# LayerNorm statistics from transposed copies with tokens on partitions

## The chip, the cores and the metric

The kernel runs on one core of a Trainium2 chip. The metric is the device time of one execution in microseconds (us). Six engines matter: PE (matrix products; its weight loads are listed apart as PEld), DVE (vector), ACT (scalar), POOL, and SP, which here only issues DMAs. Each engine works through its own queue in order; an instruction that waits holds up everything behind it on that engine.

## The reference

One inference step of a two-layer encoder over 512 prompt and 32 sample tokens, 1024 features, in float32. The part that the change touches is the end of each layer:

```python
u = x @ w_in                                   # split into three branches and three gates
...
merged = (jax.nn.sigmoid(ga) * (ya @ w_branch[0])
          + jax.nn.sigmoid(gb) * (yb @ w_branch[1])
          + jax.nn.sigmoid(gc) * (yc @ w_branch[2]))
r = ALPHA * x + merged @ w_out
r = r + jax.nn.sigmoid(r @ w_ple_gate) * (pe @ w_ple)
return layer_norm(r, ln_gain, ln_bias), ...
...
def layer_norm(x, g, b):
    mu = jnp.mean(xf, -1, keepdims=True)
    var = jnp.mean(jnp.square(xf - mu), -1, keepdims=True)
    y = (xf - mu) * lax.rsqrt(var + LN_EPS) * g + b
```

## The kernel before

Activations lie with features on partitions and tokens along the free dimension: 8 feature tiles of 128 x 544. Every float32 product is made of three products of a faster type (high and low parts of both operands: `xh`, `xl` and `wh`, `wl`), in `block` (L237), each in two halves of 272 tokens: 752 blocks of 128 x 128 weights in a layer, six matmuls each, 9,024 in all at L244. Weights come in chunks of eight blocks by DMA into `raw`; ACT and DVE split them (L200, L201), one unit ahead of PE.

The code is written out as units (`UNITS`): one unit is one feature tile of one product. Beside the units run jobs, Python generators whose `yield d` lets d ticks pass. A tick comes before each block, or before every second block where a product is made by halves. So jobs' instructions are put between matmuls at fixed places of each queue, and the numbers in `PACE` are those distances. Nothing is reordered on the chip.

A layer ends with units `wo` (output product), then `pg` (gate product), `pg` by halves from feature 6 in layer 0 and from feature 2 in layer 1 (`HELD`): first all these features for tokens 0 to 271, then all for 272 to 543. `evac` starts `gate` (L893) for each: ACT's sigmoid (L897, L899), DVE's product with `ple` (L901) and sum into r (L902). The normalization works along partitions. From the first two features PE makes a rough mean (`ln_center`, L714) that DVE and POOL subtract from all features (L718). Squares (ACT, L916) and running sums of values and squares (L918 to L928) follow. `ln_job` sums over partitions with PE (L737), makes A (power -1/2 on POOL, L745) and B on 128 partitions, spreads both over all partitions with PE (L752), and scales each feature in place (ACT L766, POOL L762, DVE L768 to L771). In layer 0 the result is split into `xh`, `xl` for layer 1, whose first units (`pl`) do not need it; in layer 1 it is stored with features on partitions (L774), and PE is given 30 and 5 matmuls on zeros (L262) around the last sums.

PSUM: two double-bank tiles for products (`mm`), two single banks `sc`, one `tp`, one `pv`.

Of the kernel before, what the change touches and what calls it, by code (L numbers as in the profile page):

```python
# [49 lines left out]
def blocks_of(kind):  # L50
# [11 lines left out]
WARM = (16, 30, 5)  # L62

PACE = {
# [53 lines left out]
def encoder(ctx: ExitStack, tc, xT, pT, W, RB, KC, VC, PAR, CST, o_y, o_k, o_v, o_rp, o_rs, o_cv, o_lr):  # L118
# [33 lines left out]
    mhalf = cp.tile([128, 3], F32, name="mhalf")  # L152
    warm = cp.tile([128, 1], F32, name="warm")
# [83 lines left out]
    def block(ps, xh, xl, first, last, hfs=(0, 1), n=None):  # L237
# [9 lines left out]
    def halves(ap):  # L247
        return ap.rearrange("p (a b) -> p a b", a=2)
# [32 lines left out]
    busy(WARM[0])  # L281
    V.memset(eps, EPS)
    V.memset(mhalf, -0.5)
    S.copy(warm, eps)
# [28 lines left out]
    def layer(l, env, nxt):  # L313
# [386 lines left out]
        def span(hf):  # L700
            return slice(0, N) if hf is None else slice(hf * H2, (hf + 1) * H2)

        def hfs_(hf):
            return (0, 1) if hf is None else (hf,)
# [4 lines left out]
        def ln_center():  # L709
            yield PACE["center"]  # L710
            c, s2 = tmp("center"), env["s2p"]
            for h in range(2):
                ps = psum("sc")
                T.matmul(ps[:, :H2], lhsT=cst[:, C_O1K:C_O1K + 128], rhs=env["acc"][:, span(h)])  # L714
                S.mul(c[:, span(h)], ps[:, :H2], 4.0)
            yield 2
            for f in (2, 3, 4, 5, 6, 7, 0, 1):
                (V if f < 4 else G).tensor_tensor(rt(f, None), rt(f, None), c, SUB)  # L718
            env["center"] = True
            yield 2  # L720
            S.activation(s2, rt(0, None), AF.Square)
            sq = tmp("sq")
            S.activation(sq, rt(1, None), AF.Square)
            yield 2
            G.tensor_tensor(s2, s2, sq, ADD)

        PIECES = [(c if i < 2 else H2 - 128, c, min(128, H2 - c), 0 if i < 2 else 128 - (H2 - c))
                  for i, c in enumerate((0, 128, 256))]

        def ln_job(hf):  # L730
            ones = cst[:, C_O1K:C_O1K + 1]
            if hf and l == L - 1:
                busy(WARM[1])
            ps = psum("tp")
            for q, src in enumerate((env["s1"], env["s2"])):
                for i, (c0, _, _, _) in enumerate(PIECES):
                    T.matmul(ps[:, 3 * q + i:3 * q + i + 1], lhsT=src[:, hf * H2 + c0:hf * H2 + c0 + 128], rhs=ones)  # L737
            if hf and l == L - 1:
                busy(WARM[2])
            w = sm.tile([128, 15], F32, tag="lnst", name="lnst", bufs=1)  # L740
            mu, e2, sq, A, B = (w[:, 3 * i:3 * i + 3] for i in range(5))
            V.tensor_copy(w[:, 0:6], ps[:, 0:6])
            V.tensor_tensor(sq, mu, mu, MUL)
            V.scalar_tensor_tensor(sq, e2, EPS, sq, ADD, SUB)
            G.tensor_tensor(A, sq, mhalf, ALU.pow)  # L745
            V.scalar_tensor_tensor(B, mu, -1.0, A, MUL, MUL)
            yield PACE[f"bc{2 * l + hf}"]
            AB = []
            for q, src in enumerate((B, A)):
                ps = psum("sc" if hf == 0 else "tp" if q == 0 else "pv")  # L750
                for i, (_, d0, n, i0) in enumerate(PIECES):
                    T.matmul(ps[:, d0:d0 + n], lhsT=bc(src[:, i:i + 1], [[0, 128]]), rhs=ident[:, i0:i0 + n])  # L752
                AB.append(ps[:, :H2])
# [340 lines left out]
```

## Time and profile before

| | us |
|---|---|
| runs | 1334.98 median of 3 (1334.26 to 1339.37) |
| profiled execution, its own time | 1333.96 |
| its span, first to last instruction | 1332.2 |
| PE / DVE / ACT / POOL busy | 1307.9 / 778.8 / 596.6 / 201.9 |

The span is what the trace covers; 1.8 us of the execution's time lie around it. A busy PE means matmuls in its pipeline, one starting about every 125 ns and each lasting about 290, so durations of matmuls overlap. The granted clock of TensorE is 1.00 at 2.4 GHz and 0.50 at 1.2 GHz; a stretch with a value between had both.

### The profile page before, as it was taken

Reading aid. Unit: us, or ns where it says so; the run is one execution under the profiler, and the core shown is the slowest. Engines: PE = TensorE matmul, PEld = TensorE weight load, DVE = VectorE, ACT = ScalarE, POOL = GpSimd, SP = SyncE. Lnnn points to the kernel's source line nnn. Section 1 sums busy time; section 2 is a strip of 40 time slices with the busy share of each in tenths; the row PEclk is TensorE's granted clock in tenths of the full one; section 3 lists DMA queues with packets and bytes.
Section 4 is the critical chain, followed back from the end, with each engine's and each line's share of the span. In section 5 each row is a group of like instructions: output and inputs, shape, how many; then the busy total and the mean of one; then the engine's idle time right before and its main releaser. Section 6 shows DMA issues by size and latency. Waiting matters only on the chain.

```text
span 1332.2 us, 26812 instructions
## 1 busy us (share of the span) xinstructions
PE 1307.9 (98%) x10783; PEld 1272.4 (96%) x10783; DVE 778.8 (58%) x1663; ACT 596.6 (45%) x1491; POOL 201.9 (15%) x192
## 2 busy tenths in 40 slices
PE   9999999999999999999999999999999999999985
PEld 9998899999999999999899998999999999999985
DVE  5666563673854444468884756547548545435587
ACT  6765544432642333334467654444245323333333
POOL 0210121320101101002312102133001110110034
PEclk9999999999999999999999999999999999999998
DMA  7233422221222222233112353232212222222201
GB/s 293 64 129 96 155 82 87 90 89 63 70 91 96 80 96 82 93 104 120 64 62 99 86 158 113 72 98 77 75 64 95 80 96 81 88 87 95 96 17 68
DMA packets 44285, 124.96 MB, mean 94 GB/s; under 512 B 9344, under 2 KB 13696, under 8 KB 43520
## 3 DMA queue, kind: packets, MB, share of 16 engines
q1 hardware_dynamic: 44160, 123.24, 28.3%
q8 instruction: 85, 1.39, 0.4%
q14 instruction: 40, 0.33, 0.1%
HBM read 111.52 MB, written 7.24 MB: 89 GB/s over the span
## 4 chain that ended last, share of the span: by engine, by line
PE 89%; DVE 6%; ACT 3%; issue 2%; POOL 0%; DVEq 0%; ACTq 0%; POOLq 0%
PE mm L244 78%; PE pv L413 2%; PE sc L386 1%; PE tp L402 1%; PE sc L639 1%; PE tp L322 1%; DVE held L201 1%; PE pv L653 1%; ACT wh L200 1%; PE mm L262 1%; DVE wl L201 1%; DVE r L718 1%; PE pv L657 1%; PE pv L497 0%; DVE s L923 0%
## 5 line engine op out<-in xcount | busy, mean ns | idle before, releaser
L201 DVE TENSOR_TENSOR wl<-raw,wh 128x256 fp32r<-128x256 f32 x704 | 306.6, 470 | 298.9 <-ACT wh L200 298.0
L244 PE MATMUL mm<-xh,wh 128*128 128x272 f32 x2144 | 455.4, 294 | 0.5 <-ACT xrp L833 0.5
L244 PE MATMUL mm<-xl,wh 128*128 128x272 f32 x2144 | 443.5, 288 | 0.0
L244 PE MATMUL mm<-xh,wl 128*128 128x272 f32 x2144 | 442.1, 287 | 0.4 <-DVE wl L201 0.4
L244 PEld LDWEIGHTS mm<-xh,wh 128*128 128x128 f32 x2144 | 334.3, 188 | 13.9 <-issue 9.9
L244 PEld LDWEIGHTS mm<-xh,wl 128*128 128x128 f32 x2144 | 335.9, 188 | 0.6 <-DVE wl L201 0.6
L244 PEld LDWEIGHTS mm<-xl,wh 128*128 128x128 f32 x2144 | 335.0, 188 | 0.0
L200 ACT CAST wh<-raw 128x256 fp32r<-128x256 f32 x704 | 251.0, 403 | 52.1 <-PE mm L244 49.3
L856 ACT ACTIVATE sg<-mm 128x544 f32<-128x544 f32 x48 | 30.0, 625 | 144.1 <-PE mm L244 144.1
L868 POOL TENSOR_TENSOR m<-m,sg 128x544 f32<-128x544 f32 x30 | 42.5, 1418 | 313.3 <-DVE sg L866 313.3
L244 PE MATMUL mm<-xh,held 128*128 128x272 f32 x320 | 64.8, 296 | 6.8 <-ACT sg L899 5.1
L347 ACT ACTIVATE sx<-sx,sst 128x128 f32<-128x128 f32 (+4 forms) x68 | 37.9, 558 | 66.7 <-DVE sst L345 63.9
L244 PEld LDWEIGHTS mm<-xh,held 128*128 128x128 f32 x320 | 51.6, 192 | 9.0 <-ACT sg L899 5.5
L244 PE MATMUL mm<-ml,wh 128*128 128x272 f32 x256 | 52.9, 288 | 0.0
L244 PE MATMUL mm<-mh,wl 128*128 128x272 f32 x256 | 52.8, 288 | 0.0
L244 PE MATMUL mm<-mh,wh 128*128 128x272 f32 x256 | 52.7, 287 | 0.0
L866 DVE TENSOR_TENSOR sg<-mm,sg 128x544 f32<-128x544 f32 x32 | 23.2, 725 | 41.3 <-PE mm L244 41.3
L255 ACT CAST xh<-r 128x544 fp32r<-128x544 f32 (+1 forms) x32 | 17.1, 533 | 66.6 <-DVE r L883 63.7
L244 PE MATMUL mm<-xl,held 128*128 128x272 f32 x160 | 46.6, 291 | 0.0
L244 PEld LDWEIGHTS mm<-mh,wl 128*128 128x128 f32 x256 | 40.1, 188 | 0.0
L244 PEld LDWEIGHTS mm<-mh,wh 128*128 128x128 f32 x256 | 40.1, 188 | 0.0
L244 PEld LDWEIGHTS mm<-ml,wh 128*128 128x128 f32 x256 | 40.0, 188 | 0.0
(257 smaller groups left out, 1855.1 us busy)
## 6 DMA issues: line engine op xcount, KB each, us to landing
raw<-in_W SPq DMA_DIRECT2D x189, 512.0 KB, 3.2
bias<-in_RB SPq DMA_DIRECT2D x16, 256.0 KB, 3.9
x<-in_xT SPq DMA_DIRECT2D x4, 544.0 KB, 8.9
o_v<-VA SPq DMA_DIRECT2D x2, 1088.0 KB, 5.6
o_k<-KT SPq DMA_DIRECT2D x2, 1088.0 KB, 5.2
swap<-KB SPq DMA_DIRECT2D x32, 68.0 KB, 2.8
swap<-QB SPq DMA_DIRECT2D x32, 68.0 KB, 2.0
o_y<-r SPq DMA_DIRECT2D x6, 272.0 KB, 2.2
```

Of the source, the lines that this page charges most:

```text
L200: S.copy(h, t)
L201: V.tensor_tensor(lo, t, h.bitcast(F32), SUB)
L244: T.matmul(ps[:, hf, :H2], lhsT=w[:, n % 2, :], rhs=x[:, hf * H2:(hf + 1) * H2], start=first and i == 0, stop=last and i == 2)
L255: S.copy(h, src)
L262: T.matmul(ps[:, 0, :H2], lhsT=zero[:, :128], rhs=zero, start=True, stop=True)
L322: T.transpose(tp[:rows, t * 128:(t + 1) * 128], src[:, t, c0:c0 + rows], ident)
L347: S.activation(x, x, AF.Exp, bias=s[:, 0:1], scale=-1.0, accum_out=s[:, 1:2])
L386: T.matmul(scs[j][:, o:o + n], lhsT=q_[r, p, i * 128:i * 128 + 128], rhs=k_[r, p, :n], start=k == 0, stop=k == 2)
L413: T.matmul(pv[64 * j:64 * j + 64, i * 128:i * 128 + 128], lhsT=env["vatok"][:, kt, h * 64:h * 64 + 64], rhs=xs[j][:, o:o + 128], start=kt ...
L856: S.activation(halves(sg), pv, AF.Sigmoid)
L866: V.tensor_tensor(halves(sg), pv, halves(sg), MUL)
L868: (V if kind == "bB" and t == 7 else G).tensor_tensor(m, m, sg, ADD)
```

## The change

Halves become tokens 0 to 287 and 288 to 543 (`SPANS`), so that they end with a token tile; the two parts lie side by side in PSUM, meeting at the bank's border. The statistics are made otherwise: PE transposes r, four feature tiles of one token tile into one `sc` bank (`turn`), and DVE takes BN_STATS over those 512 features (`stats`). That happens once per token tile for features 0 to 3 and once for 4 to 7; five token tiles, one of them with 32 tokens. BN_AGGR and one addition give mean and variance per token; POOL's power follows. Layer 0 goes on as before (A and B spread by PE, scaling with features on partitions). In layer 1 ACT also copies the transposed values to SBUF (`tk`), and the result is made from these with two scalar_tensor_tensor passes (`tok_ln`) with gain and bias spread over partitions by a DMA, and stored with tokens on partitions. For the very last token tiles features 4 to 6 are transposed and counted while the last unit runs, feature 7 after it, in banks `tp` and `pv`, and used from there. The centre, the squares, the running sums and the matmuls on zeros at the end go.

```diff
+SPANS = ((0, 288), (288, N))
+MM0 = 512 - SPANS[0][1]
+TILES = ((0, 128), (128, 256), (256, 288), (288, 416), (416, N))
+TILES_OF = ((0, 1, 2), (3, 4))
...
-WARM = (16, 30, 5)
+WARM = 16
...
+    "turn": 2, "tk": 1, "bc0": 3, "bc1": 4, "x": 5,
...
-                T.matmul(ps[:, hf, :H2], lhsT=w[:, n % 2, :], rhs=x[:, hf * H2:(hf + 1) * H2],
+                a, b = SPANS[hf]
+                T.matmul(ps[:, MM0 + a:MM0 + b], lhsT=w[:, n % 2, :], rhs=x[:, a:b],
...
-        def ln_center():
...
+        def turn(ps, c, f0, f1):
+            a, b = TILES[c]
+            for f in range(f0, f1):
+                T.transpose(ps[:b - a, f % 4 * 128:f % 4 * 128 + 128], env["r", f // 4][:, f % 4, a:b], ident)
+
+        def stats(ps, c, i, f0, f1):
+            n = TILES[c][1] - TILES[c][0]
+            V.bn_stats(bs[:n, c, i], ps[:n, f0 % 4 * 128:(f1 - 1) % 4 * 128 + 128])
+
+        def stats_job(hf, q):
+            for c in range(5) if hf is None else TILES_OF[hf]:
+                n = TILES[c][1] - TILES[c][0]
                 ps = psum("sc")
+                turn(ps, c, 4 * q, 4 * q + 4)
+                stats(ps, c, q, 4 * q, 4 * q + 4)
+                if last:
+                    env["tk", c, q] = tmp("tk", (128, 512))
+                    S.copy(env["tk", c, q][:n], ps[:n])
+                yield PACE["tk"]
+            if q:
+                add(ln_job(hf), 0)
+
+        def stats_end(t):
+            for c in TILES_OF[1]:
+                if t == 6:
+                    env["tk", c, 1] = psum("tp" if c == 3 else "pv")
+                ps = env["tk", c, 1]
+                turn(ps, c, *((4, 7) if t == 6 else (7, 8)))
+                stats(ps, c, 1 + t % 6, *((4, 7) if t == 6 else (7, 8)))
+                yield 0
+            if t == 7:
+                add(ln_job(1), 0)

         def ln_job(hf):
...
+            for i, c in enumerate(tiles):
+                n = TILES[c][1] - TILES[c][0]
+                V.bn_aggr(mv[:n, i], bs[:n, c, :3 if end else 2].rearrange("p a b -> p (a b)"))
+            V.tensor_scalar(e, mv[:, :, 1], EPS, None, ADD)
+            G.tensor_tensor(A, e, mhalf[:, :np_], ALU.pow)
+            if last:
+                yield from tok_ln(hf, tiles, mv, A, B)
+                return
+            V.scalar_tensor_tensor(B, mv[:, :, 0], -1.0, A, MUL, MUL)
+            yield PACE[f"bc{hf}"]
...
+        def tok_ln(hf, tiles, mv, A, B):
+            work = [(q, i, c) for q in range(2) for i, c in enumerate(tiles)]
...
+            for q, i, c in work:
+                n = TILES[c][1] - TILES[c][0]
+                x = env["tk", c, q][:n]
+                y = xs[q, i] = tmp("ty", (128, 512))[:n] if hf and q else x
+                V.scalar_tensor_tensor(y, x, mv[:n, i, 0:1], gain[:n, q], SUB, MUL)
+                if not hf:
                     yield 1
+            for q, i, c in work:
...
+                V.scalar_tensor_tensor(y, y, A[:n, i:i + 1], bias[:n, q], MUL, ADD)
+                Q.dma_start(out=o_y[a:b, 512 * q:512 * q + 512], in_=y)
+                if not hf:
+                    yield 1
...
             V.tensor_tensor(sg, sg, env["ple", t // 4][:, t % 4, span(hf)], MUL)
             V.tensor_tensor(r, r, sg, ADD)
...
+            if t == 3 or t == 7 and not (last and hf):
+                yield PACE["turn"]
+                add(stats_job(hf, t // 4), 0)
+            elif t in (6, 7) and last and hf:
+                add(stats_end(t), 2 * (t == 6))
...
+            if l + 1 == L and kind == "pg" and t == 0:
+                env["gb"] = sl("gb", shape=(128, 2048))
+                Q.dma_start(out=env["gb"], in_=bass.AP(LGB.tensor, LGB.offset, [[0, 128], [1, 2048]]))
```

DVE's queue at the end of layer 0, from the spreading of the first half's A to the second half's statistics. Before (`s_7685`, `s_7686` are the sums of values and squares, `lnA` is A spread):

```order
L755 COPY lnA<-sc 128x272
L768 TENSOR_TENSOR r<-r,lnA 128x272
L771 SCALAR_TENSOR_TENSOR r<-r,par_89,lnY 128x272
...
L256 TENSOR_TENSOR xl<-r,xh 128x272
L920 TENSOR_TENSOR s_7685<-s_7685,r 128x272
L923 TENSOR_TENSOR s_7686<-s_7686,sq 128x272
```

And now, the same place on DVE (`bst` takes the statistics, `lnst` mean, variance, A and B):

```order
L778 COPY lnA<-tp 128x288
L789 TENSOR_TENSOR r<-r,lnA 128x288
L790 SCALAR_TENSOR_TENSOR r<-r,par_89,lnY 128x288
L725 BN_STATS bst<-sc 128x6
L789 TENSOR_TENSOR r<-r,lnA 128x288
L790 SCALAR_TENSOR_TENSOR r<-r,par_89,lnY 128x288
L262 TENSOR_TENSOR xl<-r,xh 128x288
L725 BN_STATS bst<-sc 128x6
L790 SCALAR_TENSOR_TENSOR r<-r,par_89,lnY 128x288
L262 TENSOR_TENSOR xl<-r,xh 128x288
L760 BN_AGGR lnst<-bst 128x2 x2
L761 TENSOR_SCALAR lnst<-lnst 128x2
```

The second half's two BN_STATS and their sums now stand behind the first half's scaling steps. On PE, from the end of the first half's spreading, come 6 products, a group of four transposes, 6 products, another group, 36 products, and then the second half's spreading (L774); the products are those of `pl`, and 30 more follow.

PE's queue at the end of the kernel. Before (`zero` is the filling):

```order
L244 MATMUL mm<-xh,held 128x272
L262 MATMUL mm<-zero 128x272 x30
L737 MATMUL tp<-cst,s_15756 128x1 x3
L737 MATMUL tp<-cst,s_15757 128x1 x3
L262 MATMUL mm<-zero 128x272 x5
L752 MATMUL tp<-cst,lnst 128x128 x2
```

And now on PE, within the last unit and behind it:

```order
L253 MATMUL mm<-xh,held 128x256
L721 MATMUL tp<-cst,r 128x128 x3
L721 MATMUL pv<-cst,r 128x128 x3
L253 MATMUL mm<-xh,held 128x256
L253 MATMUL mm<-xl,held 128x256
...
L721 MATMUL tp<-cst,r 128x128
L721 MATMUL pv<-cst,r 128x128
```

Transposes of features 4 to 6 stand before the last six products, two of feature 7 behind them, and nothing of PE after that.

DVE's queue in the second half of layer 1, over its last two units. Before:

```order
L901 TENSOR_TENSOR sg<-sg,ple 128x272
L902 TENSOR_TENSOR r<-r,sg 128x272
L923 TENSOR_TENSOR s_15757<-s_15757,sq 128x272
...
L920 TENSOR_TENSOR s_15756<-s_15756,r 128x272
L923 TENSOR_TENSOR s_15757<-s_15757,sq 128x272
L742 COPY lnst<-tp 128x6
```

And now on DVE (L930 and L931 are the gate's product and sum, L814 the second pass of `tok_ln`):

```order
L814 SCALAR_TENSOR_TENSOR tk<-tk,lnst,gb 128x512
L814 SCALAR_TENSOR_TENSOR tk<-tk,lnst,gb 32x512
L930 TENSOR_TENSOR sg<-sg,ple 128x256
L931 TENSOR_TENSOR r<-r,sg 128x256
L725 BN_STATS bst<-tp 128x6
L725 BN_STATS bst<-pv 128x6
...
L807 SCALAR_TENSOR_TENSOR tk<-tk,lnst,gb 128x512 x2
L807 SCALAR_TENSOR_TENSOR ty<-tp,lnst,gb 128x512
L807 SCALAR_TENSOR_TENSOR ty<-pv,lnst,gb 128x512
```

The first half's passes now stand in front of feature 6's gate, whose sum the last unit's transposes on PE need.

## Rows read from the trace of the kernel before

**Rows 1.** The page, part 1: busy us (share of the span) xinstructions
```profile
PE 1307.9 (98%) x10783; PEld 1272.4 (96%) x10783; DVE 778.8 (58%) x1663; ACT 596.6 (45%) x1491; POOL 201.9 (15%) x192
```
**Rows 2.** Waits of PE: who waited for whom: us in total, times, longest us
```profile
PE mm L244 <- ACT sg L899: 5.1, 2, 3.1
...
PE tp L737 <- DVE s L920: 1.5, 2, 1.1
```
**Rows 3.** Stretches: length, busy us of each engine (instructions), PEclk, DMA share, GB/s
```profile
217.00:237.00 20.00, 20.00 (x167) 19.92 (x166) 8.96 (x15) 10.26 (x23) 5.76 (x5) 1.00 0.34 96
618.00:684.00 66.00, 63.03 (x477) 61.05 (x475) 56.32 (x106) 35.51 (x88) 26.54 (x24) 0.97 0.16 54
660.00:670.00 10.00, 9.61 (x67) 9.61 (x68) 7.49 (x21) 6.54 (x15) 1.80 (x3) 0.83 0.01 2
1264.00:1290.00 26.00, 22.10 (x157) 21.04 (x156) 22.78 (x40) 11.71 (x33) 10.48 (x8) 0.93 0.07 23
```
**Rows 4.** Chain of waits, 350 to 640: start us, us, what
```profile
355.87 261.80 PE mm L244 x2088
617.67 0.92 PE sc L714 x4
```
**Rows 5.** PE's timeline, first of six L497: start, us, engine line op, names, shapes
```profile
44.50 0.29 PE L497 MATMUL sc<-xch,held 128*128 128x274 f32 x1
...
45.26 0.42 PE L244 MATMUL mm<-xh,wh 128*128 128x272 f32 x2
```
**Rows 6.** PE's timeline at an existing group of four transposes
```profile
219.47 0.60 PE L322 MATMUL tp<-cst,VB 128*128 128x128 f32 x4
219.83 0.50 PE L244 MATMUL mm<-xh,wh 128*128 128x272 f32 x2
220.16 0.41 PE L244 MATMUL mm<-xl,wh 128*128 128x272 f32 x2
```
**Rows 7.** PE's timeline, sums over partitions and spreading, layer 1, first half
```profile
1293.11 1.45 PE L737 MATMUL tp<-cst,s 128*128 128x1 f32 x12
...
1297.51 1.41 PE L752 MATMUL sc<-cst,lnst 128*128 128x128 f32 x12
```
**Rows 8.** PE's timeline, two waits and the last product (idle before, releaser)
```profile
1280.40 0.47 PE L244 MATMUL mm<-xh,held 128*128 128x272 f32 x1 [3.12 <-ACT sg L899]
...
1309.24 0.39 PE L244 MATMUL mm<-xh,held 128*128 128x272 f32 x1 [1.95 <-ACT sg L899]
...
1312.24 0.29 PE L244 MATMUL mm<-xh,held 128*128 128x272 f32 x1
```
**Rows 9.** Groups of DVE by form: count | busy us, mean ns | idle before
```profile
L487 DVE SCALAR_TENSOR_TENSOR xc<-xrp,par,xc 128x547 f32<-128x547 f32 x24 | 18.9, 787 | 4.1 <-ACT xc L485 3.5
L352 DVE TENSOR_SCALAR sx<-sx,sst 128x512 f32<-128x512 f32 x16 | 9.4, 590 | 0.6
L418 DVE COPY ya<-pv 128x512 f32<-128x512 f32 x8 | 5.5, 688 | 5.2 <-PE pv L413 5.2
L744 DVE SCALAR_TENSOR_TENSOR lnst<-lnst 128x3 f32<-128x3 f32 x4 | 0.7, 164 | 0.1
```
**Rows 10.** Timeline of POOL and DVE, layer 0's first half being scaled
```profile
654.02 5.67 POOL L762 TENSOR_TENSOR r<-r,lnA 128x272 f32<-128x272 f32 x6 [0.77 <-DVE lnA L755]
654.53 0.82 DVE L771 SCALAR_TENSOR_TENSOR r<-r,par,lnY 128x272 f32<-128x272 f32 x1
657.14 1.00 DVE L768 TENSOR_TENSOR r<-r,lnA 128x272 f32<-128x272 f32 x1
```
**Rows 11.** Timeline of ACT, DVE and POOL behind the last product
```profile
1314.03 0.38 ACT L899 ACTIVATE sg<-mm 128x272 f32<-128x272 f32 x1
1315.21 0.44 DVE L902 TENSOR_TENSOR r<-r,sg 128x272 f32<-128x272 f32 x1
1318.85 0.86 POOL L745 TENSOR_TENSOR lnst<-lnst,mhalf 128x3 f32<-128x3 f32 x1 [4.32 <-DVE lnst L744]
1325.15 3.96 DVE L771 SCALAR_TENSOR_TENSOR r<-r,par,lnY 128x272 f32<-128x272 f32 x7
```

More of the change, by code (lines that the diff above doesn't have):

```diff
@@ L280, in encoder @@
     V.memset(zero.bitcast(F32), 0.0)
-    busy(WARM[0])
+    busy(WARM)
     V.memset(eps, EPS)
     V.memset(mhalf, -0.5)
+    V.memset(lnst, 0.0)
     S.copy(warm, eps)
@@ L700, in span @@
         def span(hf):
-            return slice(0, N) if hf is None else slice(hf * H2, (hf + 1) * H2)
-        def hfs_(hf):
-            return (0, 1) if hf is None else (hf,)
+            return slice(0, N) if hf is None else slice(*SPANS[hf])
+        last = l == L - 1
         def rt(f, hf):
             return env["r", f // 4][:, f % 4, span(hf)]
-        def ln_center():
-            yield PACE["center"]
-            c, s2 = tmp("center"), env["s2p"]
-            for h in range(2):
-                ps = psum("sc")
[L714 to L725, printed above, removed]
@@ L727, in layer @@
-        PIECES = [(c if i < 2 else H2 - 128, c, min(128, H2 - c), 0 if i < 2 else 128 - (H2 - c))
-                  for i, c in enumerate((0, 128, 256))]
-        def ln_job(hf):
[L731 to L747, printed above, removed]
+        bs = bst[:, l]
@@ new lines, in stats_end @@
+        def stats_end(t):
[8 more added lines that the diff above has]
+                add(ln_job(1), 0)
+        def ln_job(hf):
+            tiles = TILES_OF[hf]
+            end = last and hf
+            np_ = len(tiles)
+            w = lnst[:, l, hf]
+            mv, e, A, B = w[:, :2 * np_].rearrange("p (a b) -> p a b", b=2), w[:, 6:6 + np_], w[:, 9:9 + np_], w[:, 12:12 + np_]
+            for i, c in enumerate(tiles):
[8 more added lines that the diff above has]
+            yield PACE[f"bc{hf}"]
@@ L748, in ln_job @@
             AB = []
+            first = SPANS[hf][0]
             for q, src in enumerate((B, A)):
[L750 to L753, printed above, removed]
+                ps = psum("sc" if hf else "tp" if q else "pv")
+                for i, c in enumerate(tiles):
+                    a, b = TILES[c]
+                    T.matmul(ps[:, a - first:b - first], lhsT=bc(src[:b - a, i:i + 1], [[0, 128]]),
+                             rhs=ident[:b - a, :b - a])
+                AB.append(ps[:, :SPANS[hf][1] - first])
@@ L756, in ln_job @@
             yield 1
-            last = l + 1 == L
-            while hf and not last and ("x", 7, 0) not in nxt:
+            while hf and ("x", 7, 0) not in nxt:
                 yield 1
-            pooled = range(3, 8) if last and hf else range(2, 8)
-            for f in pooled:
+            for f in range(2, 8):
                 G.tensor_tensor(rt(f, hf), rt(f, hf), A, MUL)
@@ L779, in ln_job @@
                     nxt["x", e, hf] = True
-                if not last:
-                    yield 1 + f % 2
-                elif not hf:
+                yield 1 + f % 2
+        def tok_ln(hf, tiles, mv, A, B):
+            work = [(q, i, c) for q in range(2) for i, c in enumerate(tiles)]
+            gain, bias = (env["gb"][:, k * 1024:k * 1024 + 1024].rearrange("p (a b) -> p a b", a=2) for k in range(2))
+            xs = {}
+            for q, i, c in work:
[6 more added lines that the diff above has]
+            for q, i, c in work:
+                a, b = TILES[c]
+                n = b - a
+                y = xs[q, i]
+                V.scalar_tensor_tensor(y, y, A[:n, i:i + 1], bias[:n, q], MUL, ADD)
+                Q.dma_start(out=o_y[a:b, 512 * q:512 * q + 512], in_=y)
+                if not hf:
                     yield 1
@@ L875, in evac @@
                     env["ple", t // 4] = sl("ple")
-                S.copy(halves(env["ple", t // 4][:, t % 4]), pv)
+                S.copy(env["ple", t // 4][:, t % 4], pv)
             elif kind == "wo":
@@ L895, in gate @@
             sg = tmp("sg")[:, span(hf)]
-            if hf is None:
-                S.activation(halves(sg), ps[:, :, :H2], AF.Sigmoid)
-            else:
-                S.activation(sg, ps[:, hf, :H2], AF.Sigmoid)
+            S.activation(sg, ps[:, MM0:MM0 + N][:, span(hf)], AF.Sigmoid)
             yield 1
```

84 lines of the change are left out of this document (26 added, 58 removed), and 1 row of the table PACE.

## The prediction

> **What bounds the kernel now.** I read the engine shares first, then TensorE's waits, then busy time and granted clock by stage, then the timeline of the slow places. PE is busy 1307.9 of the 1332.2 us span [rows 1], so outside a few stretches time is what PE must issue, plus where it stands. It stands longest, 5.1 us, for the gate's sigmoid (L899, in layer 1) and 1.5 us for a running sum (L920, in layer 0) [rows 2]. Both belong to the end-of-layer normalization, and that is where all the slack lies: over 618 to 684 us PE is busy 63.03 of 66 us, so 3.0 idle, and over 1264 to 1290 us 22.10 of 26, so 3.9 idle; and the granted clock is 0.83 over 660 to 670 and 0.93 over 1264 to 1290 us [rows 3], which is 0.17 x 10 = 1.7 us and 0.07 x 26 = 1.8 us of full-speed time (part of the latter while PE stands; I count 1.5). And from the end of the last product (1312.24 + 0.29 = 1312.53, [rows 8]) to the end of the span lie 19.7 us in which one chain over all engines runs: filling matmuls, sums, power, broadcast, eight features in place, stores.
>
> **The change, part by part.**
> *PE work.* Added: 80 transposes, 18 groups of four (10 in layer 0, 8 in layer 1) before the last eight. An old group of four starts at 219.47, the next product at 219.83, and that pair then takes 0.33 instead of 0.25 us [rows 6]: 0.36 + 0.08 = 0.44 us a group, 18 x 0.44 = 7.9 us. Removed: the mean's matmuls, 0.92 us a layer [rows 4], 1.8; the twelve passes of sums, 1.45 us [rows 7], three times before the tail, 4.4; the broadcast's twelve passes of layer 1's first half, 1.4 [rows 7]; four of the twelve passes of layer 0's second half, 0.5. Sum 8.1. Net **-0.2 us**.
>
> *The split 288 + 256 for 272 + 272.* All 9,024 products (4,512 pairs) change shape. 2,088 products of 272 columns take 261.80 us, 125.4 ns each [rows 4]; six of 274 take 45.26 - 44.50 = 0.76 us, 127 ns [rows 5]. So a column costs, and 288 + 256 cost what 544 cost before: **0**. Bounds: were the time set by columns alone it would be exactly 0 (a gain has no source); were 256 columns held at the pace of 272 (no row shows fewer columns under a full 128x128 load of this type) and 288 paid 125.4 x 16/272 = 7 ns more, the price is 4,512 x 7 ns = 32 us. Matmuls with one column, whose pace only the weight load can set, start every (1.45 - 0.25)/11 = 109 ns [rows 7], the last pass taken at 0.25 us, below the 118 ns expected for 256. I take 0, by that nearest row.
> The Trainium skill ("TensorE: Matmul & The Clock Gate", LDWEIGHTS (loading the stationary operand)) gives a weight load as its columns over 1.2 ns, 107 ns for 128, which is also what 256 columns take at 2.4 GHz: no slack is left, which speaks against this split. The 109 ns agrees with it; by the page the load just still hides, and the sum stays.
>
> *Layer 0.* The subtraction of the centre goes (4 on DVE, 4 on POOL), squares and running sums too; ten BN_STATS of 512 columns come, not in the trace. Nearest row: a DVE copy of 128x512 from PSUM, 688 ns [rows 9]; bounds 0.59 (the same width as tensor_scalar from SBUF, [rows 9]) and 1.4 (two such passes). I take 0.69. Lost before: 3.0 idle + 1.7 clock = 4.7 us. What is late next: PE's second broadcast (L774; here L774, L789, L790 and L262 are lines of the new code). From the end of the first one PE issues 48 products and two groups of transposes, 48 x 0.125 + 0.88 = 6.9 us. DVE in that time, in its queue order: copy of A 0.44, L789 0.44, L790 0.82, BN_STATS 0.69, L789 1.0, L790 0.82, L262 1.0, BN_STATS 0.69, L790 0.49, L262 0.43; POOL's six multiplications make the two-operand ones that slow (0.82 and 1.00 between 654.02 and 659.69, [rows 10]). With 0.3 us to begin, 7.1 us; two BN_AGGR and the addition at the length of other tiny operations (0.16, [rows 9]) 0.5; the power 0.86 [rows 11] and two handovers 0.4; B 0.2; so 9.2 us. PE stands 2.3 to 2.8 us, taken as 2.8, and I count another 1.5 us for a clock drop as behind the wait of 3.12 us. With 0.4 for small waits that stay, 4.7 against 4.7: **0**. Queued behind it on PE: 30 products for ple, then layer 1's first; nothing else waits.
>
> *Layer 1, first half.* The sigmoid stood in ACT's queue behind a square that waited for the centre's subtraction: 3.12 us at 1280.40 [rows 8], most of the 3.9 idle. No centre, no such wait; with the clock 1.5 that is 5.4; I leave 0.4 for new waits on a DVE that still splits weights. **-5.0 us**.
>
> *Layer 1, second half.* The 1.95 us at 1309.24 [rows 8] go the same way. New: DVE applies the first half's normalization, twelve scalar_tensor_tensor over 512 columns (a 32-row tile costs as much). The row of this form, 547 columns with a column operand, is 787 ns [rows 9]; 0.75 for 512. From the first tile's statistics (24 x 0.118 + 0.44 + 0.3 = 3.6 us after the half begins) to feature 6's sum DVE has 5 x 0.69 + 5 gates x 0.9 (product and sum, [rows 11]) + 0.7 small + 12 x 0.75 = 17.7 us: done at 21.4 with 0.1 of gaps. PE reaches feature 6's transposes after 138 products of 118 ns and five groups: 18.5 us. It stands **2.9** us, with 18 of the last unit's products done and 6 queued behind, and six more transposes cost 0.75. -1.95 + 2.9 + 0.75 = **+1.7 us**.
>
> *The tail.* From the last product: sigmoid 0.42, product and sum 0.96 [rows 11], two transposes 0.44, two BN_STATS of 128 columns 0.48, two BN_AGGR and one addition 0.5: 2.8 us. Then eight passes of 0.75 = 6.0; the power (0.86) runs beside the first four. The last store: before, DVE ended at 1325.15 + 3.96 = 1329.11 [rows 11], 3.1 us ahead of the span's end; four stores of 256 KB follow each other now, so 3.5. Sum 12.3 against 19.7: **-7.4 us**.
>
> *At nothing:* the load of gain and bias (1 MB) sits in SP's queue between weight loads that come once per 6 us unit; three follow it. ACT's eight copies replace eight squares and eight lnY. If that cover fails, one weight load is about 3 us late.
>
> Sum: -0.2 + 0 + 0 - 5.0 + 1.7 - 7.4 = -10.9 us against the profiled execution's 1333.96 (span 1332.2): 1323.1. The median of the runs is 1.0 higher, so about **1323 to 1324; I say 1323.5**.
>
> **Rivals.**
> 1. *Slower: 256 columns no longer hide the weight load.* Place: every pair. At the bound of 32 us the time is 1334 - 11 + 32 = 1355. It decides from 4 ns a pair (18 us: 1341). For it: no row below 272; against: 109 ns above. 0.08.
> 2. *No change: VectorE is the bound at the end.* BN_STATS at 1.4 us: five in the second half (+3.5), two at the layer boundary (+1.4), 2 x 0.2 in the tail, and feature 6 late by as much again where POOL or ACT hand over late: +6, 1329 to 1330. For it: DVE is loaded in both stretches; against: single-operand reads from PSUM are 688 ns. 0.12.
> 3. *Faster still: DVE keeps up,* neither new wait appears (2.9 + 2.5 + 1.5): 1316 to 1317. For it: my queue sums carry small gaps; against: twelve passes of 0.75 do not shrink. 0.20.
> 4. *The transposes cost clock.* If groups between products count as idling, the clock halves at the four clusters, 1.5 us each: +6, 1329. Against: 217 to 237 us hold five such groups at a clock of 1.00 [rows 3]. The Trainium skill (same page, Part 4: PE-mode transpose) says that the full clock does not engage for transposes, since they do not count as busy; the trace does not bear that out for groups between products. 0.05.
>
> Forecast (both new waits as above, within some 3 us): 0.55.
>
> **How the numbers follow.** Predicted 1323.5, the forecast's own range 1320 to 1328. The range holds rival 3 (low end 1314, with passes at 0.69 as well) and most of rivals 2 and 4, and 1 or 2 ns a pair: 1314 to 1332. Measurement tells from no change about 0.5%, here 6.7 us: faster is below 1328.3, slower above 1341.7. Faster: 0.55 + 0.20 + 0.02 of rivals 2 and 4 = 0.77; same 0.15; slower 0.08.
>
> **What the profile after would show.** PE: pairs of 288 and 256 starting 0.25 us apart together; groups of four transposes 0.36 us long; a wait of 2 to 3 us before layer 0's second broadcast, with a clock below 1 behind it; no wait for the sigmoid; about 3 us before feature 6's transposes. DVE: BN_STATS of 512 near 0.69 us, passes near 0.75. Last product to end: about 12 us instead of 19.7. The prediction is wrong if pairs take more than 254 ns, if PE waits for the statistics' PSUM buffers (DVE late by more than two tiles), or if the tail stays above 15 us.

## The result

The kernel after takes 1319.38 us (median of four runs, 1318.69 to 1319.66), the kernel before 1336.37 us (median of four, 1334.26 to 1339.37): a ratio of 0.987, 95% interval 0.985 to 0.989. The profiled executions went from 1333.96 to 1319.27 us, 14.7 us less where the working said 10.9, and their spans from 1332.2 to 1317.2. The medians lie 17.0 us apart, since executions of the kernel before vary more, from 1333.94 us at a mean granted clock of 0.993 to 1339.61 at 0.988 (the four of the kernel after have 0.996 or 0.997), and the profiled one is among the fastest. Faster was right. The time lies in the stated range of 1314 to 1332, 0.6 us below the forecast's own 1320 to 1328, between the forecast and rival 3. The sum was 4 us short, and single terms were off by up to 3.4 us, because some errors cancel.

### The profile page after: what moved, and what is told of

It is laid out like the page before. It is cut to its first block, busy times and chain, and to the rows that moved or that the text cites. A ratio compares the mean times of both kernels' runs of the same rounds, so it can differ in the third digit from the quotient of the medians.

```text
span 1317.2 us, 26576 instructions
## 1 busy us (share of the span) xinstructions
PE 1299.4 (99%) x10744; PEld 1265.1 (96%) x10744; DVE 757.1 (57%) x1649; ACT 581.5 (44%) x1447; POOL 164.4 (12%) x158
## 4 chain that ended last, share of the span: by engine, by line
PE 81%; DVE 4%; ACT 2%; issue 1%; DVEq 0%; POOL 0%; ACTq 0%
PE mm L253 72%; PE pv L420 1%; PE tp L409 1%; PE sc L393 1%; PE sc L646 1%; PE tp L329 1%; PE pv L660 1%; PE pv L664 1%; PE sc L583 0%; ACT wh L208 0%; PE sc L721 0%; PE sc L476 0%; DVE tk L807 0%; DVE tk L814 0%; DVE xl L262 0%
## 5 line engine op out<-in xcount | busy, mean ns | idle before, releaser
L253 PE MATMUL mm<-xh,wh 128*128 128x288 f32 x2144 | 457.9, 295 | 0.4 <-ACT xrp L866 0.4
L253 PE MATMUL mm<-xh,wl 128*128 128x288 f32 x2144 | 444.1, 288 | 0.0
L253 PE MATMUL mm<-xl,wh 128*128 128x288 f32 x2144 | 442.7, 288 | 0.0
L253 PEld LDWEIGHTS mm<-xh,wl 128*128 128x128 f32 x2144 | 328.6, 188 | 0.0
L208 ACT CAST wh<-raw 128x256 fp32r<-128x256 f32 x704 | 251.0, 403 | 53.1 <-PE mm L253 49.3
L253 PE MATMUL mm<-xh,held 128*128 128x288 f32 (+1 forms) x320 | 64.0, 291 | 0.3 <-ACT ple L908 0.3
L253 PE MATMUL mm<-mh,wh 128*128 128x288 f32 (+1 forms) x256 | 52.8, 288 | 0.0
L253 PE MATMUL mm<-mh,wl 128*128 128x288 f32 (+1 forms) x256 | 52.8, 287 | 0.0
L253 PE MATMUL mm<-ml,wh 128*128 128x288 f32 (+1 forms) x256 | 52.8, 287 | 0.0
L253 PE MATMUL mm<-xl,held 128*128 128x288 f32 (+1 forms) x160 | 46.4, 290 | 0.5 <-DVE xl L262 0.4
L261 ACT CAST xh<-r 128x544 fp32r<-128x544 f32 (+2 forms) x32 | 17.0, 531 | 67.5 <-DVE r L915 63.5
```

What stands on the lines that cost most here:

```text
L208: S.copy(h, t)
L253: T.matmul(ps[:, MM0 + a:MM0 + b], lhsT=w[:, n % 2, :], rhs=x[:, a:b], start=first and i == 0, stop=last and i == 2)
L261: S.copy(h, src)
```

## The profile after

The page of the kernel after, part 1 (busy us, share of the span, instructions), to lay beside [rows 1]:

```profile
PE 1299.4 (99%) x10744; PEld 1265.1 (96%) x10744; DVE 757.1 (57%) x1649; ACT 581.5 (44%) x1447; POOL 164.4 (12%) x158
```

PE is busy 8.5 us less in a span 15 us shorter. The waits of PE in the kernel after, to lay beside [rows 2]:

```profile
PE tp L721 <- DVE r L931: 2.0, 2, 1.4
PE sc L774 <- DVE lnst L766: 1.5, 1, 1.5
...
PE mm L253 <- DVE xl L262: 0.4, 1, 0.4
```

The sigmoid is gone from the list. Both waits that the prediction expected in its place are there, each shorter than forecast: before layer 0's second broadcast (L774) 1.5 us for 2.8, and before feature 6's transposes 0.6 for 2.9 (the other 1.4 of L721 is in the tail, where PE has only feature 7's transposes left). In PE's timeline:

```profile
665.36 1.16 PE L774 MATMUL sc<-cst,lnst 128*128 128x128 f32 x8 [1.47 <-DVE lnst L766]
...
1304.74 0.33 PE L721 MATMUL tp<-cst,r 128*128 128x128 f32 x1 [0.61 <-DVE r L931]
```

The stretches of [rows 3], in the kernel after:

```profile
217.00:237.00 20.00, 20.00 (x165) 19.94 (x165) 9.13 (x14) 9.38 (x21) 4.39 (x4) 1.00 0.36 110
618.00:684.00 66.00, 63.66 (x502) 62.16 (x500) 45.19 (x103) 31.40 (x77) 12.69 (x14) 1.00 0.18 58
660.00:670.00 10.00, 8.53 (x70) 8.31 (x69) 8.62 (x21) 7.92 (x18) 5.81 (x8) 1.00 0.00 1
1264.00:1290.00 26.00, 26.00 (x206) 25.93 (x205) 16.14 (x38) 10.83 (x31) 0.00 (x0) 1.00 0.09 32
```

The sixth figure from the left behind the length is the granted clock: it is 1.00 in all four rows, and the 0.83 and 0.93 of the kernel before are gone. The last row also holds three groups of four transposes between products. The Trainium skill ("TensorE: Matmul & The Clock Gate", Part 4: PE-mode transpose) says that the full clock does not engage for transposes; for groups of four among products this trace shows the clock at 1.00.

To see where the time went I cut both traces at the same four products. PE's timeline of the kernel before, at the start of layer 0's first gate product, of layer 1's first product over both halves and of layer 1's first gate product (the last product is in [rows 8]):

```profile
598.72 0.42 PE L244 MATMUL mm<-xh,wh 128*128 128x272 f32 x2
...
684.69 0.52 PE L244 MATMUL mm<-xh,wh 128*128 128x272 f32 x2 [0.46 <-ACT xrp L833]
...
1252.10 0.41 PE L244 MATMUL mm<-xh,wh 128*128 128x272 f32 x2
```

The same three and the last product in the kernel after:

```profile
600.89 0.41 PE L253 MATMUL mm<-xh,wh 128*128 128x288 f32 x2
...
684.34 0.52 PE L253 MATMUL mm<-xh,wh 128*128 128x288 f32 x2 [0.41 <-ACT xrp L866]
...
1252.80 0.42 PE L253 MATMUL mm<-xh,wh 128*128 128x288 f32 x2
...
1305.84 0.28 PE L253 MATMUL mm<-xh,held 128*128 128x256 f32 x1
```

The table gives the five pieces, in us of the profiled executions, for these two kernels and those of the experiments below. A and C hold no normalization, B is the boundary of the layers, D the last gate units, E the tail from the last product's start. Where the code of a piece is the same, A differs between kernels by up to 1.7 us, B to E by 0.7 at most.

| kernel | A: to 1st gate | B: to layer 1 | C: to 2nd gate | D: to last product | E: to the end | span |
|---|---|---|---|---|---|---|
| before | 598.7 | 86.0 | 567.4 | 60.1 | 19.9 | 1332.2 |
| after | 600.9 | 83.4 | 568.5 | 53.0 | 11.4 | 1317.2 |
| e1 split only | 599.9 | 87.7 | 568.8 | 60.9 | 18.8 | 1336.1 |
| e2 no centre | 599.5 | 86.0 | 567.5 | 53.0 | 19.7 | 1325.7 |
| e3 no token form | 600.6 | 83.4 | 568.4 | 56.6 | 16.4 | 1325.4 |
| e4 broadcast later | 600.8 | 83.7 | 568.9 | 53.1 | 11.4 | 1317.8 |
| e5 broadcast earlier | 600.4 | 86.4 | 568.4 | 53.1 | 11.4 | 1319.6 |
| e6 double statistics | 601.6 | 83.4 | 568.4 | 56.2 | 11.5 | 1321.0 |
| e7 all at the end | 599.9 | 83.5 | 569.1 | 51.6 | 12.2 | 1316.2 |
| e8 wide 272 | 598.9 | 83.3 | 567.8 | 53.0 | 11.4 | 1314.4 |
| e9 e7 and e8 | 599.0 | 83.3 | 568.3 | 51.5 | 12.2 | 1314.3 |
| e10 one column | 600.4 | 86.6 | 569.1 | 53.0 | 11.5 | 1320.6 |

## The experiments

**e1 and e8: what the split costs.** e1 gives the kernel before the columns 288 and 256:

```diff
-                T.matmul(ps[:, hf, :H2], lhsT=w[:, n % 2, :], rhs=x[:, hf * H2:(hf + 1) * H2],
+                a, b = SPANS[hf]
+                T.matmul(ps[:, MM0 + a:MM0 + b], lhsT=w[:, n % 2, :], rhs=x[:, a:b],
...
-            pv = ps[:, :, :H2]
+            pv = ps[:, MM0:MM0 + N]
```

> The kernel before with one part of the change alone: products cut into 288 and 256 columns (and the product's PSUM buffer read as one stretch of 544 columns); the old statistics stay, cut at column 288 too. My step: the split costs nothing, at most 3 us in all (0.65 ns for each of 4,512 pairs, which is what the milestones of the two traces leave for it), so 1336 to 1339 us, with pairs starting 0.250 to 0.252 us apart. Rival 1 of the prediction: 256 columns no longer hide the weight load, 7 ns a pair, +32 us, about 1368. The second half of the last layer has six passes fewer (the broadcast needs two pieces of tokens, not three), which is worth 0.5 us.

Measured: 1338.82 against 1336.12 us, a ratio of 1.0017 (1.0006 to 1.0027), 0.8 to 3.6 us slower. Rival 1 with its 32 us is dead, but the term is not 0. In the profiles e1 is 3.9 us longer, and that is not all the split's price: A and C hold 2.6 of it, and 1.7 are in B, where the old sums over partitions now stand behind a longer wait and the clock falls once more. Twelve passes of one column behind a wait of PE, first in e1, then in the kernel before, each with a stretch of 5 us around them:

```profile
649.77 1.50 PE L741 MATMUL tp<-cst,s 128*128 128x1 f32 x12 [0.66 <-DVE s L924]
650.00:655.00 5.00, 5.00 (x32) 5.00 (x32) 2.16 (x8) 0.42 (x1) 1.62 (x2) 0.66 0.00 0
```

```profile
648.34 1.50 PE L737 MATMUL tp<-cst,s 128*128 128x1 f32 x12 [0.35 <-DVE s L920]
648.00:653.00 5.00, 4.66 (x39) 4.66 (x40) 2.20 (x9) 1.04 (x4) 1.38 (x2) 1.00 0.00 0
```

The clock at 0.66 over 5 us costs 0.34 x 5 = 1.7 us. e8 gives the kernel after equal halves again wherever both halves run at once:

```diff
-                a, b = SPANS[hf]
-                T.matmul(ps[:, MM0 + a:MM0 + b], ...
+                (a, b), m0 = (SPANS[hf], MM0) if len(hfs) == 1 else ((hf * H2, hf * H2 + H2), 512 - H2)
+                T.matmul(ps[:, m0 + a:m0 + b], ...
...
```

> The kernel after, but all products that run over both halves at once are cut 272 and 272 again; 288 and 256 are kept where the two halves are computed one after the other (the last six features of layer 0 and six of layer 1, and the first two products of layer 1). The split alone was 2.7 us slower than the kernel before (0.8 to 3.6). Theory A: that is the price of a pair of unequal columns, in every pair; it comes back: 2 to 2.5 us faster than the kernel after, 1316.5 to 1317.5, and layer 1 from its first wide product to its first gate takes 567.4 us in place of 568.5. Theory B: the price sits in the stretches by halves, and in other code: no change, 1319.

Measured: 1316.41 us (1316.17 to 1316.81), 3.0 below the kernel after, ratio to before 0.986 (0.984 to 0.987); A and C fall by 2.0 and 0.7. Theory A is right in its sign and about in its size. The long runs of products in the chain of waits (start, us) show the part that lies in the pairs themselves, first of the kernel after, then of e8:

```profile
357.79 270.44 PE mm L253 x2154
...
1009.97 264.61 PE mm L253 x2106
```

```profile
356.00 270.07 PE mm L253 x2154
...
1007.18 264.51 PE mm L253 x2106
```

That is 0.47 us over 4,260 products, or about 1 us over all 9,024 at this rate. The start times of the products in A give more. From PE's 241st product (37.51 us in the kernel after) to the first gate product, the four kernels with equal halves (before, e2, e8, e9) take 561.7 us each, and those with 288 and 256 columns 562.7 to 562.8; only the kernel after and e4 have 563.4, because a group of transposes at 168 us (L409) comes 0.6 us late in them. So the split costs 1.0 us there, and 0.6 to 0.8 in C (after against e8, e7 against e9). e7 and e9, which differ in the split alone, lie 1.9 us apart in span: I take that as its price. The rest of e8's 3.0 is that late group and PE's first 240 products, which differ by up to 1.7 us between kernels with the same code there. Why an unequal pair costs more stays open.

**e2: the centre.** Layer 1 of the kernel before without its first centre (the mean lacks two features there):

```diff
-            for h in range(2):
+            for h in range(2 if l + 1 < L else 0):
...
-            for f in (2, 3, 4, 5, 6, 7, 0, 1):
+            for f in (2, 3, 4, 5, 6, 7, 0, 1) if l + 1 < L else ():
```

> The kernel before, with the first centre left out in layer 1 alone: neither its four matmuls nor the eight subtractions, the squares stay (so the mean lacks two features there). My step: the centre's subtraction held the square, which held the sigmoid on ACT, for which PE stood 5.1 us; without it PE's waits for the sigmoid go (under 0.5 us in all), the granted clock over 1264 to 1290 us is 1.00, 0.9 us of matmuls go: 6 to 8 us faster, 1328.5 to 1330.5. Rival: the waits come from a VectorE that is also splitting weights, and from ACT's queue itself; then the sigmoid is as late as before and only the matmuls go: 1 us faster, about 1335.

Measured: 1327.32 us, ratio 0.993 (0.991 to 0.995); in the profiles the span is 6.5 us shorter and D 7.1, all of it in the first half. The waits of PE and the stretch 1264 to 1290 in e2:

```profile
PE mm L244 <- ACT sg L899: 2.0, 1, 2.0
```

```profile
1264.00:1290.00 26.00, 26.00 (x211) 26.00 (x210) 19.21 (x46) 12.38 (x35) 6.03 (x6) 1.00 0.11 37
```

The first half's wait and its clock drop were the centre's, as claimed. The second half's 1.95 us stays, so it was not the centre's. ACT's timeline in e2 shows what holds it:

```profile
1301.24 0.43 ACT L916 ACTIVATE sq<-r 128x272 f32<-128x272 f32 x1 [4.24 <-DVE r L902]
1301.58 1.03 ACT L766 ACTIVATE lnY<-sc,par 128x272 f32<-128x272 f32 x2
1302.50 0.39 ACT L899 ACTIVATE sg<-mm 128x272 f32<-128x272 f32 x1
```

A square stands in ACT's queue ahead of the sigmoid and waits for the sum on DVE, which is busy scaling the first half. The kernel after has no squares, so this wait goes too, by another cause than the one written down.

**e3: the token form.** The kernel after with layer 1 finished feature by feature again:

```diff
-            if last:
-                yield from tok_ln(hf, tiles, mv, A, B)
-                return
...
+                    if last and f in (1, 3, 5, 6, 7):
+                        f0 = f - (f < 6)
+                        Q.dma_start(out=o_y[:, f0:f + 1, span(hf)], in_=...)
```

> The kernel after with the second part of the change undone: layer 1 takes its statistics from turned copies, but is normalized feature by feature with broadcasts, and stored, as before. My step: the statistics shorten the tail by some 3 us and the token form by the rest. Behind the last product: sigmoid, sums, transposes, statistics 2.8 us as now; power and handovers 1.2; from the power's end to VectorE's end 9.4 us as in the trace of before (1319.71 to 1329.11); 3.1 to the end of the span: 16.5 us against 11.1 now, +5.4. The first half's broadcasts cost PE 1.4 us more, and feature 6's wait of 0.6 us goes: about 6 us slower than the kernel after, 1325 to 1326. Rival: the statistics (and the removed filling matmuls) carry the tail's gain, and the token form only moves VectorE's work: within 1.5 us of the kernel after, 1318 to 1321.

Measured: 1327.55 us, ratio to before 0.993 (0.991 to 0.995), 8.2 us slower than the kernel after. The tail was about as worked out (E 16.4, which is 16.1 behind the product's end where I expected 16.5), so of the tail's 8.5 us the statistics, with the filling gone, are worth 3.5 and the token form 5.0. D was not: 3.6 us longer where I expected 0.8. The first half's broadcasts are 1.4 of it, as counted; in PE's timeline of e3 two waits stand that I had not expected:

```profile
1297.25 0.66 PE L721 MATMUL sc<-cst,r 128*128 128x128 f32 x4 [0.55 <-DVE lnA L775]
...
1307.93 0.33 PE L721 MATMUL tp<-cst,r 128*128 128x128 f32 x1 [1.26 <-DVE r L937]
```

Feature 6 is later here (a wait of 1.26 us for 0.61), though DVE has less to do. In DVE's timeline of e3 it stands idle where the token form kept it busy, and longest for the spreading on PE:

```profile
1296.73 0.46 DVE L775 COPY lnA<-sc 128x288 f32<-128x288 f32 x1 [2.70 <-PE sc L771]
```

Another 0.98 us it waits for POOL's power; and beside POOL's multiplications (1297.34 to 1302.76) a product of two tensors took up to 1.06 us there. How much each adds to the 1.26 was not tested. Some 1.0 us of the 3.6 is not accounted for (3.6 - 1.4 - 0.55 - 0.65).

**e4, e5 and e10: the wait at the boundary, and the clock.** e4 and e5 move layer 0's second broadcast some 12 products back or forward, e10 adds passes of one column behind it:

```diff
-    "turn": 2, "tk": 1, "bc0": 3, "bc1": 4, "x": 5,
+    "turn": 2, "tk": 1, "bc0": 3, "bc1": 6, "x": 5,      # e4
+    "turn": 2, "tk": 1, "bc0": 3, "bc1": 2, "x": 5,      # e5
...
+                if hf and q == 0:                            # e10
+                    for _ in range(12):
+                        T.matmul(ps[:, 300:301], lhsT=ident, rhs=ident[:, 0:1])
```

> The kernel after with layer 0's second broadcast issued some 12 products later (a pace of 6 in place of 4), so that PE does not stand 1.47 us before it. Theory A: VectorE, which runs without a gap from 657 to 683 us, sets when layer 1's first products have their x; PE then waits as much longer for xl behind the broadcast (0.40 us at 680.55 now): no change, within 0.5 us. Theory B: PE's own queue sets the end there, and the 1.5 us are gained: 1318.

Measured: 1318.85 us (1318.84 to 1319.80), no change. The wait of 1.47 us is gone, and some 0.9 of it come back within 14 us as waits that are shorter or absent in the kernel after (0.31 at 670.94, 0.40 at 680.55). In PE's timeline of e4 the three longest are:

```profile
670.10 0.40 PE L253 MATMUL mm<-xh,held 128*128 128x288 f32 x1 [0.49 <-ACT ple L908]
...
679.25 0.39 PE L253 MATMUL mm<-xl,held 128*128 128x256 f32 x1 [0.42 <-DVE xl L262]
680.65 0.39 PE L253 MATMUL mm<-xl,held 128*128 128x256 f32 x1 [0.43 <-DVE xl L262]
```

B is 83.7 for 83.4, and DVE's last split of x (L262) begins 81.7 us behind the first gate product in the kernel after and 81.9 in e4: theory A, DVE sets the end of B, and the wait of 1.47 us costs nothing by itself.

> The kernel after with layer 0's second broadcast issued some 12 products (1.5 us) earlier (a pace of 2 in place of 4), so that PE stands about 3.0 us before it and not 1.47. My step in the prediction: a wait of some 2.8 us costs the granted clock another 1.5 us. If so the clock falls below 1 behind the wait (over 664 to 672 us) and layer 1 begins up to 1.5 us later. Rival: what fell in the kernel before was the clock behind standing followed by twelve passes of one column; behind standing alone, with passes of 128 columns after it, it stays at 1.00, and since VectorE sets the end of this stretch the time does not change (within 0.5 us of 1319).

Measured: 1321.49 us (1321.27 to 1321.78), 2.1 slower. PE's timeline at the wait, and the stretches of 2 us behind it:

```profile
664.84 1.73 PE L774 MATMUL sc<-cst,lnst 128*128 128x128 f32 x8 [2.95 <-DVE lnst L766]
```

```profile
664.00:666.00 2.00, 1.16 (x7) 1.16 (x8) 0.96 (x3) 0.00 (x0) 0.59 (x1) 0.81 0.00 0
666.00:668.00 2.00, 2.00 (x11) 2.00 (x11) 0.42 (x1) 0.00 (x0) 0.89 (x2) 0.50 0.00 0
668.00:670.00 2.00, 2.00 (x15) 2.00 (x15) 0.84 (x1) 1.92 (x4) 2.00 (x4) 0.84 0.02 4
```

The wait is twice as long, and behind it the clock goes to half (1.2 GHz) for some us, which costs 2 x (0.19 + 0.50 + 0.16) = 1.7 us. B becomes 86.4, somewhat longer than the 86.0 of the kernel before. So the step "a wait of 2.8 us costs 1.5 us of clock" was right to 0.2 us; the wait in the kernel after was not that long.

> The kernel after with twelve extra matmuls of one column behind the wait of 1.47 us before layer 0's second broadcast (they write columns that nothing reads), like the twelve of the kernel before behind its wait of 1.13 us, where the clock fell to 0.50. Theory A: to the clock, passes of one column are as good as standing; 1.5 us of standing and 1.3 us of them make the clock fall as 2.95 us of standing did: below 1 over 664 to 670 us, and the kernel is 2 to 3 us slower (1321.5 to 1322.5). Theory B: any matmul keeps the clock; it stays at 1.00, the passes cost their 1.3 us at most (1319.4 to 1320.7), and what fell in the kernel before had another cause.

Measured: 1323.40 us (1321.80 to 1325.54). The twelve became 24 passes (each fp32 matmul is two), so they cost 2.6 us and not 1.3, and the time lies above theory A's 1321.5 to 1322.5. PE's timeline and the stretches in e10:

```profile
664.83 0.71 PE L774 MATMUL sc<-cst,lnst 128*128 128x128 f32 x4 [1.47 <-DVE lnst L766]
665.37 2.74 PE L779 MATMUL sc<-cst 128*128 128x1 f32 x24
```

```profile
668.00:670.00 2.00, 2.00 (x14) 2.00 (x15) 0.42 (x1) 0.41 (x1) 0.80 (x2) 0.78 0.00 0
670.00:672.00 2.00, 2.00 (x11) 2.00 (x10) 1.27 (x2) 1.02 (x3) 2.00 (x3) 0.50 0.00 0
672.00:674.00 2.00, 2.00 (x16) 2.00 (x15) 1.11 (x2) 1.45 (x4) 1.86 (x3) 0.87 0.00 0
```

In the kernel after, eight passes of 128 columns and then products stand behind the same wait of 1.47 us, and the clock stays at 1.00; in e10, with 24 passes of one column among them, it falls to 0.50. That fits the kernel before at 660 us, where it fell behind 1.13 us of standing and twelve such passes. Without a wait ahead of them twelve passes cost the kernel before no clock: those at 1293.11 [rows 7] lie in this stretch of it:

```profile
1290.00:1300.00 10.00, 10.00 (x85) 10.00 (x84) 5.21 (x15) 2.72 (x7) 2.17 (x3) 1.00 0.01 2
```

So twelve such passes cost clock behind 0.66 us (e1) and 1.13 us of standing and none behind 0.35 us (both shown under e1) or behind no wait. Twelve behind 1.47 us were not tried.

**e6: is DVE the bound of the second half?**

```diff
                 stats(ps, c, q, 4 * q, 4 * q + 4)
+                if last and c > 2 - 3 * q and hf is not None:
+                    stats(ps, c, q, 4 * q, 4 * q + 4)
```

> The kernel after with five BN_STATS of 128x512 in layer 1 issued twice (the three of the first half's last features, the two of the second half's first), all of them ahead of feature 6's sum on VectorE: 5 x 0.62 = 3.1 us more there, the idle 0.45 us at 1289.4 taken off. Theory A (the forecast's: VectorE sets when feature 6's transposes go): the wait before them grows from 0.61 to some 3.2 us, and the time by about 2.6 us, to 1322; if the clock falls behind so long a wait, 1 to 1.5 more. Theory B (rival 3: VectorE keeps up): the wait grows by less than 1 us, 1319 to 1320.

Measured: 1322.43 us (1321.41 to 1322.84); D is 3.1 us longer for 3.1 us more on DVE. The wait before feature 6 grew to 1.78 us, less than the 3.2 I said, but PE now also waits for the sigmoid and for ACT's copies:

```profile
1291.48 0.61 PE L721 MATMUL sc<-cst,r 128*32 128x128 f32 x4 [0.35 <-ACT tk L737]
...
1301.08 0.39 PE L253 MATMUL mm<-xh,held 128*128 128x256 f32 x1 [0.68 <-ACT sg L930]
...
1308.43 0.33 PE L721 MATMUL tp<-cst,r 128*128 128x128 f32 x1 [1.78 <-DVE r L933]
```

The time is theory A's: in this stretch a us more on DVE is a us at the end.

**e7 and e9: the early part of the last statistics.** e7 turns and counts features 4 to 7 together behind the last product; e9 is e7 with e8:

```diff
...
-                turn(ps, c, *((4, 7) if t == 6 else (7, 8)))
-                stats(ps, c, 1 + t % 6, *((4, 7) if t == 6 else (7, 8)))
+                turn(ps, c, 4, 8)
+                stats(ps, c, 1, 4, 8)
...
-            elif t in (6, 7) and last and hf:
+            elif t == 7 and last and hf:
```

> The kernel after without the early part of the last statistics: the second half's features 4 to 7 are turned and counted together behind the last product, where now 4 to 6 go ahead of it. Gained before the last product: the wait of 0.61 us and six transposes of about 0.12 us, 1.3 us. Lost behind it: six more transposes, 0.7, and two BN_STATS of 512 for two of 128 columns, 0.62 against 0.28 a piece, of which one lies beside the transposes, 0.4 to 0.7. Both together: within 0.5 us of the kernel after. Rival: the early part hides its whole cost, and leaving it out loses 1.3 us or more (1320.5).

> The kernel after with both edits that were faster alone: wide products cut 272 and 272 (1316.4 us), and the last statistics all behind the last product (1317.8). Theory A: the two lie in different stretches and add up; from the last gate unit to the end the second was worth 0.6 us, so about 1315.8. Theory B: the second one's 1.6 us of median were chance between runs, and nothing comes on top: 1316.4.

Measured: e7 1317.81 us (1316.86 to 1318.28); D falls by 1.5 and E rises by 0.8, a gain of 0.7 in all, just beyond the 0.5 expected; the rival (1.3 us lost) is out. The medians differ by more, 1.6; in the profiles A, whose code is the same, was 1.0 shorter too. e9: 1316.30 us, ratio to before 0.985 (0.983 to 0.986). It beats the kernel after by 3 us, but cannot be told from e8's 1316.41; D and E are 0.7 shorter, A and C 0.6 longer, and the latter is within what pieces of the same code differ by.

## Why the prediction came out as it did

The working's terms, put on the five pieces (the PE work on the piece where it lies), against the traces:

| piece | predicted | measured | why |
|---|---|---|---|
| A and C (split) | 0 | +3.2 | not free: 1.7 by e7 against e9; the rest differs between executions |
| B (layer 0, with +0.1 of PE work) | +0.1 | -2.5 | wait 1.47, not 2.8; no clock drop |
| D, first half (-5.0, +0.4 of PE work) | -4.6 | -4.8 | the centre (e2), and wider products |
| D, second half (+1.7, -0.65 of PE work) | +1.05 | -2.3 | wait 0.61, not 2.9, and narrower products |
| E (tail) | -7.4 | -8.5 | eight passes 5.4 us, not 6.0; store 3.1, not 3.5 |

D's halves are cut where the second half's products begin, at 1289.35 before and 1285.26 after. The split moves 1.1 us from the second half to the first: 144 products of 288 columns start 0.133 us apart and 144 of 256 columns 0.118, where 272 columns took 0.125. The working has this in no term. Without it the first half gains 5.9 and the second 1.2.

Most mechanisms held: no wait for the first half's sigmoid, two new waits where they were named, the clock behind a long wait, the tail's chain. The second half's 1.95 us went for another reason than the one given (e2), so that term came out by luck. What failed is the size of DVE's queue, most of all in the second half and in the tail. DVE's groups by form in the kernel after:

```profile
L725 DVE BATCH_NORM_STATS2 bst<-sc 128x6 f32<-128x512 f32 x14 | 9.7, 694 | 6.4 <-PE sc L721 6.4
...
L814 DVE SCALAR_TENSOR_TENSOR tk<-tk,lnst,gb 128x512 f32<-128x512 f32 x6 | 4.3, 744 | 0.0
```

Both durations are those that I took (0.69 and 0.75). But the timeline in the second half shows their spacing (first the half's first product on PE, then DVE):

```profile
1285.26 0.28 PE L253 MATMUL mm<-xh,held 128*128 128x256 f32 x1
...
1296.42 0.68 DVE L725 BATCH_NORM_STATS2 bst<-sc 128x6 f32<-128x512 f32 x1
1297.03 0.72 DVE L807 SCALAR_TENSOR_TENSOR tk<-tk,lnst,gb 32x512 f32<-32x512 f32 x1
1297.68 0.68 DVE L725 BATCH_NORM_STATS2 bst<-sc 128x6 f32<-128x512 f32 x1
...
1299.06 2.72 DVE L814 SCALAR_TENSOR_TENSOR tk<-tk,lnst,gb 128x512 f32<-128x512 f32 x4
...
1304.26 0.43 DVE L931 TENSOR_TENSOR r<-r,sg 128x256 f32<-128x256 f32 x1
```

Four passes take 2.72 us, so one begins 0.66 after the other: an instruction's record runs on 0.08 us into the next one's. Twelve passes are 8.0 us and not 9.0, five BN_STATS 3.1 and not 3.45, five gates 4.0 and not 4.5, the tail's eight passes 5.4 and not 6.0. Feature 6's sum ended 1304.69 - 1285.26 = 19.4 us into the half, and not 21.4. PE came to that place 18.9 us into it, and not 18.5, because two transposes of features 4 and 5 go ahead: a wait of 0.6 us and not 2.9. The Trainium skill ("Perfetto Trace Analysis", Optimizing Scalar/DVE Operations) says that part of a profiled latency, the write's acknowledgement, overlaps with the next instruction; these rows agree, by 0.08 us a piece.

At the boundary the working's 9.2 us from the first broadcast to B were 8.5, by other terms. DVE's timeline and POOL's there:

```profile
658.97 0.61 DVE L790 SCALAR_TENSOR_TENSOR r<-r,par,lnY 128x288 f32<-128x288 f32 x1 [1.13 <-ACT lnY L787]
...
664.40 0.70 POOL L762 TENSOR_TENSOR lnst<-lnst,mhalf 128x2 f32<-128x2 f32 x1 [1.19 <-DVE lnst L761]
```

A wait of 1.13 us for ACT, which the working did not have, took back what closer spacing and one operation of 0.45 us in place of 1.0 gained; the power and its two handovers took 0.8 us and not 1.26. PE's own 6.9 us were 7.0, so it stood 1.47, where the working had 2.3 and took 2.8. And that wait was the wrong place to price the stretch: "nothing else waits" behind it failed, since with the wait gone (e4) PE waits for DVE's splits of x instead.

So the main failing step is "twelve passes of 0.75 do not shrink", with which I held rival 3 down. Rival 3 was half true: both waits stayed, at half (1.47 of 2.8) and a fifth (0.61 of 2.9) of their size. Rival 2 had the right place (e6) and the wrong duration. The split was put at the lower of its bounds by the nearest row, one-column passes every 109 ns; that row speaks against rival 1's 32 us, and says nothing of the 1.9 us that unequal pairs brought. The total came within 4 us partly by luck: the 3.2 us that A and C lost hid as much of the gain elsewhere.

## What to carry to other kernels

Add up a queue of short vector instructions by the distance of their starts in a run of them, not by their recorded durations; here that was 0.08 us each, and a wait forecast at 2.9 us came out at 0.6. Price a wait of PE in two parts, the standing and the clock behind it, and ask whether another engine sets the end of the stretch anyway: 1.47 us before the second broadcast cost no clock, and taking them away gained nothing (e4); 2.95 us at the same place cost 1.7 us of clock (e5). Where only some stretches need an uneven cut, cut only there (e8).

## What the runs showed of the hardware that I had not expected

- The clock fell to 0.50 after 1.47 us of standing, four passes of 128 columns and 2.6 us of one-column passes (e10); it stayed at 1.00 where eight passes of 128 columns and products stood behind the same wait (the kernel after). Twelve one-column passes were followed by a fall behind 0.66 us of standing (e1) and by none behind 0.35 us (the kernel before).
- In the kernel after BN_STATS over 512 columns takes 0.68 us on 32 partitions and 0.69 on 128; 128 columns take 0.28 to 0.30.
- Pairs of 288 and 256 columns are slower than 272 and 272 by some 0.2 ns a pair in the long runs, and by 1.9 us, 0.4 ns a pair, between e7 and e9, which differ in nothing else; the medians of e1 say 2.7 us (0.8 to 3.6). Why is unexplained.
